# Low parts of q as 128-row operands, and the next pair's stacked operands begun in closer steps

## The chip, the cores and the metric

The kernel runs on one core of one Trainium2 chip. The metric is the device time of one execution in microseconds (us); lower is better. Times shown are medians of several runs. A profile is one further execution with the hardware profiler on; its times are in us from the first instruction.

## The reference, cut to what matters

The reference is one layer of a streaming encoder on 512 prompt frames of one stream and 16 new frames for each of 8 running streams: 640 columns in all, model width 1024. One combined projection gives the input of a state-space branch, q, k, v and two gates. The state-space branch and an attention branch are merged, projected and added to x; a gated feed-forward block with a short convolution follows, then a last norm.

The change lies in the prompt half of the attention: 8 heads of 64 channels, 512 queries. A chunk of 64 queries reads its own and all earlier chunks:

```python
sc = jnp.einsum('nihd,nkhd->nhik', qc, kb).astype(jnp.float32) * scale + bias
sc = jnp.where(valid, sc, MASK_VALUE)
p = jax.nn.softmax(sc, axis=-1).astype(v.dtype)
return jnp.einsum('nhik,nkhd->nihd', p, vb)
```

## The kernel before, in words

**Precision.** TensorE multiplies operands in a reduced fp32 format. To keep fp32 accuracy an operand is split into a high part (ACT rounds it) and a low part (DVE subtracts the high part from the original). A product is then high times high, high times low and low times high.

**Main work and side work.** All instructions are issued in an order fixed when the program is built. The projections run in slots of 8 ticks; one tick is 6 matmuls of 128 rows, 128 columns of weights and 320 moving columns (`mm3`, all of them on line 115). At a slot's first tick the weights three slots on are loaded (`load`, line 100, on SP's queue), the next weights are split on ACT (line 107), and two ticks later on DVE (line 112). The result of the slot before leaves PSUM on DVE (line 1046 for the gates). Ahead of each tick's matmuls a few steps of side work are issued; a rate, `side[2]`, sets how many, about two per tick in the attention. The side work is the state-space branch (`s5`) and then `attention`.

**Attention.** Heads are worked in four pairs. `attention` writes a plan: a list of functions for each step, run in order of step. A pair takes 32 steps. For a pair that begins at step t0, the scores of the eight query blocks (4 tiles of 128 queries, 2 heads) are due at t0, 3, 6, 9, 16, 19, 22 and 25 (`prompt`, function `a`); normalisation follows 4 steps later (`n`, lines 731 and 732), transposes 8 later (`b`, line 738), the product with v 12 after a tile's second head (`prompt_pv`). The running streams' attention (`sample`) is due at steps 12 and 28: its scores (line 786), transposes 8 on (line 802), product with cached v 12 on (line 814). One step after a sample's scores the cached k and v of the next sample are loaded (`load_kv`, lines 769 and 773, three buffers each), on SP's queue. The position bias of the next pair (`load_pb`, line 709, two buffers) is loaded at steps 23 and 26.

**Scores.** A head has 64 channels, so an operand fills 64 of the 128 rows. `stacks` builds, for the next pair, tiles in which the 128 rows are used for two products at once: `ks[:, h2]` holds the high part of k in the head's own 64 rows and its low part in the other 64; `qs[:, h2]` holds the high part of q in both. One 128-row matmul then gives high times high plus high times low. The low part of q lies in `ql` (64 rows of it for each head) and a second matmul of 64 rows adds low times high. Both write PSUM bank `sS`, of which there is one; DVE adds the bias and takes the maximum from it (line 725), after which the next scores may overwrite it. ACT takes the exponent (line 693).

**Building the stacks.** Four functions: the high part of k on ACT (line 663); its low part on DVE (line 668); the copy of that low part to the other 64 rows by two DMAs on SP's queue (line 672), with the high part of q on ACT; the copy of q's high part to the other rows by two DMAs, with q's low part on DVE. They are called at steps 13, 17, 21 and 25 of a pair. For the first pair they run inside `s5`, one in each of its last four rounds.

**SP's queue** issues DMAs in program order; one that waits for a buffer holds those behind it.

At the start of `attention` GpSimd clears `QB` (line 840), a tile for the running streams' q, and DVE copies into it (line 844, two copies in each of four steps), before step 0.

Of the kernel before, what the change touches and what calls it, by code (L numbers as in the profile page):

```python
# [8 lines left out]
F32 = mybir.dt.float32  # L9
F32R = mybir.dt.float32r  # L10
I32 = mybir.dt.int32
AF = mybir.ActivationFunctionType
OP = mybir.AluOpType
# [30 lines left out]
def body(nc, tc, d, ctx):  # L44
# [8 lines left out]
    V, A, G, PE, S = nc.vector, nc.scalar, nc.gpsimd, nc.tensor, nc.sync  # L53
# [3 lines left out]
    def nm(s):  # L57
        uid[0] += 1
        return f"{s}{uid[0]}"

    def ht(dt=F32, w=T):
        return heap.tile([128, w], dt, tag="T", name=nm("h"))
# [4 lines left out]
    def smps(tag):  # L67
        return pss.tile([128, 512], F32, tag=tag, name=nm(tag))
# [45 lines left out]
    def mm(ps, lhs, rhs, start, stop):  # L114
        PE.matmul(ps, lhs, rhs, start=start, stop=stop)  # L115
# [149 lines left out]
    def s5():  # L265
# [359 lines left out]


        first = stacks(0)
        for q in range(4):
            w = w2_ops(q + 2) if q < 2 else []
# [11 lines left out]
    vt_, qT, kT, yh, att = [], [], [], [], []  # L641

    qk = [None]

    def half(h2):
        return slice(64 * h2, 64 * h2 + 64)

    st_ = {}

    def stacks(hp):  # L650


        if hp > 3:
            return []
        k, q, ql = (qk[0].tile([128, n, 512], F32R, tag=t, name=nm(t), bufs=2)
                    for t, n in (("ks", 2), ("qs", 2), ("ql", 1)))
        kl = ht(F32R, 512).rearrange("p (a b) -> p a b", a=1)
        st_[hp] = (k, q, ql)

        def hi(dst, src):  # L660
            for h2 in range(2):
                s = half(h2)
                A.activation(dst[s, h2, :], src[s, 0:512], AF.Copy)

        def lo(dst, src, h):
            for h2 in range(2):
                s = half(h2)
                V.tensor_tensor(dst[s, 0, :], src[s, 0:512], h[s, h2, :].bitcast(F32), op=OP.subtract)

        def move(dst, src):  # L670
            for h2 in range(2):
                S.dma_start(dst[half(1 - h2), h2, :].bitcast(F32), src(h2).bitcast(F32))
        return [lambda: hi(k, kT[hp]), lambda: lo(kl, kT[hp], k),
                lambda: (move(k, lambda h2: kl[half(h2), 0, :]), hi(q, qT[hp])),
                lambda: (move(q, lambda h2: q[half(h2), h2, :]), lo(ql, qT[hp], q))]

    def attention():
        st = ExitStack()
        ap_ = st.enter_context(tc.tile_pool(name="attn", bufs=2))
# [4 lines left out]
        def evac(o, i):  # L684
            cnt[0] += 1
            if cnt[0] % 2:
                A.activation(o, i, AF.Copy)
            else:
                V.tensor_copy(o, i)

        def exps(sb, w, mx):
            V.tensor_scalar(mx[:, 2:3], mx[:, 1:2], -1.0, None, op0=OP.mult)  # L692
            A.activation(sb[:, :w], sb[:, :w], AF.Exp, bias=mx[:, 2:3], accum_out=mx[:, 3:4])  # L693
            return sb

        def tiles():
            sb = ap_.tile([128, T], F32, tag="e", name=nm("sb"), bufs=4)
            mx = ap_.tile([128, 8], F32, tag="mx", name=nm("mx"), bufs=6)
            return sb, mx

        def at(t, fn):
            plan.setdefault(t, []).append(fn)
# [3 lines left out]
        def load_pb(h):  # L706
            if h < 8:
                pbs[h] = ap_.tile([128, 512], F32, tag="pb", name=nm("pb"))
                S.dma_start(pbs[h], d["pbias"][h])

        def prompt(t0, h, t):
            hp, h2 = h // 2, h % 2
            w = 128 * (t + 1)
            s = half(h2)
            m = {}

            def a():
                sc = smps("sS")
                k, q, ql = st_[hp]
                n = max(w, 256)  # L720
                ts = slice(128 * t, 128 * t + 128)
                mm(sc[:, :n], q[:, h2, ts], k[:, h2, 0:n], True, False)
                mm(sc[:, :n], ql[s, 0, ts], k[s, h2, 0:n], False, True)
                sb, mx = tiles()
                V.tensor_tensor_reduce(sb[:, :w], sc[:, :w], pbs[h][:, 512 - w:512], 1.0, -3.0e38,
                                       op0=OP.add, op1=OP.max, accum_out=mx[:, 1:2])
                m["e"], m["mx"] = exps(sb, w, mx), mx

            def n():
                e, mx = m["e"], m["mx"]  # L730
                V.reciprocal(mx[:, 4:5], mx[:, 3:4])
                V.tensor_scalar(e[:, :w], e[:, :w], mx[:, 4:5], None, op0=OP.mult)

            def b():
                e = m["e"]
                pt = smps("sT")
                for k in range(t + 1):
                    PE.transpose(pt[:, k * 128:k * 128 + 128], e[:, k * 128:k * 128 + 128], ident)  # L738
                m["eT"] = ap_.tile([128, 512], F32, tag="eT", name=nm("eT"), bufs=3)
                evac(m["eT"][:, :w], pt[:, :w])  # L740

            at(t0, a)
            at(t0 + 4, n)
            at(t0 + 8, b)
            return m

        def prompt_pv(t0, hp, t, ms):

            def c():
                if t == 0:  # L750
                    po[0] = smps("sP")
                for k in range(t + 1):
                    for h2, m in enumerate(ms):
                        h = 2 * hp + h2
                        mm(po[0][half(h2), 128 * t:128 * t + 128], vt_[k][:, h * 64:h * 64 + 64],
                           m["eT"][:, k * 128:k * 128 + 128], k == 0, k == t)
                if t == 3:
                    evac(att[hp][:, 0:512], po[0])

            at(t0, c)  # L760

        def load_kv(hp, g4):
            if g4 == 0:
                sbs[hp] = ap_.tile([128, 576], F32, tag="sbias", name=nm("sbias"), bufs=1)
                S.dma_start(sbs[hp], d["sbias"][hp])
            kc, vc = [], []
            for i in range(2):
                k = ap_.tile([128, 2, 512], F32, tag="kc", name=nm("kc"), bufs=3)
                S.dma_start(k, d["kc"][hp, g4, :, 2 * i:2 * i + 2])
                kc.append(k)  # L770
            for i in range(2):
                v = ap_.tile([128, 2, 4, 128], F32, tag="vc", name=nm("vc"), bufs=3)
                S.dma_start(v, d["vc"][hp, g4, :, 2 * i:2 * i + 2])
                vc.append(v)
            kvs[hp, g4] = (kc, vc)
# [65 lines left out]
        for hp in range(4):  # L841
            for h2 in range(2):
                s = slice(64 * h2, 64 * h2 + 64)
                V.tensor_copy(QB[s, hp, :, h2, :], qT[hp][s, 512:640].rearrange("p (n i) -> p n i", n=8))
            yield

        t0 = 0
        nxt = [None]
        for hp in range(4):
            for t in range(4):  # L850
                ms = []
                for h2 in range(2):
                    ms.append(prompt(t0, 2 * hp + h2, t))
                    if t == 3:
                        at(t0 + 1, lambda h=2 * hp + h2: load_pb(h + 2))
                    t0 += 3
                    if t == 1 and h2 == 1:
                        at(t0, lambda hp=hp: nxt.__setitem__(0, stacks(hp + 1)))
                        for j in range(4):
                            at(t0 + 1 + 4 * j, lambda j=j: nxt[0] and nxt[0][j]())  # L860
                prompt_pv(t0 - 3 + 12, hp, t, ms)
                if t % 2:
                    i = 2 * hp + t // 2
                    sample(t0, hp, t // 2)
                    if i < 7:
                        at(t0 + 1, lambda i=i: load_kv((i + 1) // 2, (i + 1) % 2))
                    t0 += 4
# [29 lines left out]
    def side_work():  # L897
        qk[0] = qctx.enter_context(tc.tile_pool(name="qk", bufs=1))
        yield from s5()
        side[2] = 172 / (247 - clock[0])  # L900
        yield from attention()
        qctx.close()
# [148 lines left out]
    n = 0  # L1051
# [74 lines left out]
    h2 = xctx2.enter_context(tc.tile_pool(name="heap2", bufs=1))  # L1126
# [298 lines left out]
    for p, nf in enumerate(PARTS):  # L1425
        for j in range(nf):
            f = f0 + j
            q = len(segs)
# [52 lines left out]
    q = len(segs)  # L1481
# [244 lines left out]
```

## Time and profile before

| what | value |
|---|---|
| median of 3 runs | 951.29 us (951.09 to 952.75) |
| profiled execution | 955.98 us, span 953.9 us from first to last instruction |
| mean granted TensorE clock in it | 0.985 of full speed |
| PE busy | 923.4 us, 97% of the span |
| DVE, ACT, POOL busy | 628.0, 442.1 and 133.4 us |
| HBM read, written | 114.56 MB, 8.21 MB |

A row of the timeline is the start in us, the duration in us, the engine, the line, the operation with its output and inputs, for matmuls rows\*columns of the weights and then partitions x moving columns, and how many alike were merged. In brackets stand the idle time of that engine just before and what ended it. Matmuls are pipelined: the step from one start to the next is their price, not their duration.

### The profile page before, as it was taken

How to read it: one execution, taken by the hardware profiler on the slowest of the kernel's cores; microseconds unless marked ns; L12 is line 12 of the kernel's file. 1: busy time of each engine (PE TensorE's matmuls, PEld its weight loads, DVE VectorE, ACT ScalarE, POOL GpSimd, SP SyncE). 2: the span in 40 equal slices, each digit the busy share in tenths (PEclk: the TensorE clock that was granted, in tenths of full speed). 3: DMA queues.
4: the chain of work that ended last, by engine and by line, in shares of the span. 5: the costliest groups of instructions: out<-in, count | busy, mean ns of one | idle time of the engine just before them, and what ended most of it. 6: DMA issues, size and time to landing. Idle time of an engine off the chain costs nothing.

```text
span 953.9 us, 16515 instructions
## 1 busy us (share of the span) xinstructions
PE 923.4 (97%) x6534; PEld 875.8 (92%) x6534; DVE 628.0 (66%) x1261; ACT 442.1 (46%) x689; POOL 133.4 (14%) x228
## 2 busy tenths in 40 slices
PE   8999999999999999999998989999999999999995
PEld 8978999977777799999998989999999999999994
DVE  6783996474665543566777877766766676666545
ACT  6244113343333364433667445545455545555441
POOL 0120403200000000000003212212122211222100
PEclk9999999999999999999999999999999999999998
DMA  6744329666647522234538778889878888899833
GB/s 223 198 137 125 133 68 110 216 199 215 169 129 230 159 81 67 72 105 158 136 84 178 156 165 188 206 186 200 196 178 187 201 191 180 197 191 192 189 57 110
DMA packets 62428, 151.76 MB, mean 159 GB/s; under 512 B 20944, under 2 KB 24208, under 8 KB 62352
## 3 DMA queue, kind: packets, MB, share of 16 engines
q1 hardware_dynamic: 45392, 95.90, 33.3%
q0 software_dynamic: 16096, 54.03, 29.9%
q8 instruction: 51, 0.84, 0.4%
q10 hardware_dynamic: 864, 0.78, 0.2%
q14 instruction: 25, 0.20, 0.1%
HBM read 114.56 MB, written 8.21 MB: 129 GB/s over the span
## 4 chain that ended last, share of the span: by engine, by line
PE 79%; DVE 7%; DMA 6%; ACT 4%; issue 2%; SPq 0%; DVEq 0%; ACTq 0%
PE pb L115 46%; PE sS L115 10%; PE sX L115 8%; PE sT L115 7%; PE sP L115 5%; DMA wl<-in_w 3%; DMA qs<-qs 2%; PE sT L738 1%; DMA fl<-s 1%; PE sX L814 1%; DVE h L1524 1%; DMA wr<-in_w 1%; DVE h L1198 1%; DVE tmp L1356 1%; PE sS L786 1%
## 5 line engine op out<-in xcount | busy, mean ns | idle before, releaser
L115 PE MATMUL pb<-h,wh 128*128 128x320 f32 (+2 forms) x2000 | 389.3, 316 | 4.9 <-ACT h L944 1.8
L115 PEld LDWEIGHTS pb<-h,wh 128*128 128x128 f32 x2000 | 314.2, 190 | 14.3 <-issue 6.6
L115 PE MATMUL pb<-h,wl 128*128 128x320 f32 (+2 forms) x1000 | 231.9, 311 | 0.4 <-DVE wl L112 0.4
L115 PEld LDWEIGHTS pb<-h,wl 128*128 128x128 f32 x1000 | 168.8, 189 | 0.9 <-DVE wl L112 0.7
L1288 POOL DMA_DIRECT2D fl<-s x41 | 35.7, 871 | 455.4 <-PE pb L115 271.8
L107 ACT ACTIVATE wh<-wr 128x1024 fp32r<-128x1024 f32 x50 | 52.7, 1054 | 82.0 <-PE pb L115 55.9
L112 DVE TENSOR_TENSOR wl<-wr,wh 128x1024 fp32r<-128x1024 f32 x50 | 61.1, 1221 | 39.5 <-ACT wh L107 39.3
L115 PE MATMUL sS<-h,wh 128*128 128x320 f32 x336 | 75.6, 312 | 0.0
L115 PE MATMUL sX<-h,fh 128*128 128x320 f32 x320 | 71.7, 312 | 0.0
L1286 ACT ACTIVATE fl<-s 128x1024 fp32r<-128x1024 f32 x41 | 43.3, 1057 | 56.3 <-PE sT L115 48.8
L693 ACT ACTIVATE sb<-sb,mx 128x128 f32<-128x128 f32 (+4 forms) x40 | 24.2, 605 | 73.7 <-DVE mx L692 49.0
L115 PEld LDWEIGHTS sS<-h,wh 128*128 128x128 f32 x336 | 57.0, 190 | 0.0
L115 PE MATMUL sS<-h,wl 128*128 128x320 f32 x168 | 53.0, 316 | 3.1 <-DMA wl<-in_w 3.1
L115 PEld LDWEIGHTS sX<-h,fh 128*128 128x128 f32 x320 | 54.2, 190 | 0.0
L1288 POOL DMA_DIRECT2D wl<-in_w x43 | 38.1, 887 | 87.0 <-ACT wl L1286 79.8
L115 PE MATMUL sX<-h,fl 128*128 128x320 f32 x160 | 49.8, 311 | 0.0
L1359 ACT ACTIVATE tmp<-tmp 128x512 f32<-128x512 f32 x22 | 13.9, 633 | 76.0 <-DVE tmp L1356 76.0
L1286 ACT ACTIVATE wl<-wr 128x1024 fp32r<-128x1024 f32 (+1 forms) x43 | 43.5, 1012 | 7.3 <-PE sS L115 6.2
L115 PE MATMUL sT<-h,gh 128*128 128x320 f32 x176 | 40.0, 315 | 4.5 <-DVE u L1445 4.5
L1287 ACT ACTIVATE wh<-wr 128x1024 fp32r<-128x1024 f32 (+1 forms) x43 | 43.1, 1003 | 0.0
L1287 ACT ACTIVATE fh<-s 128x1024 fp32r<-128x1024 f32 x41 | 42.9, 1046 | 0.0
L1356 DVE SCALAR_TENSOR_TENSOR tmp<-tmp,vec 128x656 f32<-128x656 f32 x44 | 39.5, 898 | 0.7
(338 smaller groups left out, 1684.2 us busy)
## 6 DMA issues: line engine op xcount, KB each, us to landing
wr<-in_w SPq DMA_DIRECT2D x112, 512.0 KB, 4.7
fl<-s POOLq DMA_DIRECT2D x41, 512.0 KB, 6.0
wl<-in_w POOLq DMA_DIRECT2D x39, 512.0 KB, 8.4
kc<-in_kc SPq DMA_DIRECT2D x16, 512.0 KB, 6.4
vc<-in_vc SPq DMA_DIRECT2D x16, 512.0 KB, 5.7
x<-in_x SPq DMA_DIRECT2D x7, 320.0 KB, 6.4
pb<-in_pbias SPq DMA_DIRECT2D x8, 256.0 KB, 7.4
h<-in_x SPq DMA_DIRECT2D x6, 320.0 KB, 4.5
```

Source lines behind the costliest of these rows:

```text
L107: A.activation(hi, raws[u], AF.Copy)
L112: V.tensor_tensor(lo, raws[u], hi.bitcast(F32), op=OP.subtract)
L115: PE.matmul(ps, lhs, rhs, start=start, stop=stop)
L693: A.activation(sb[:, :w], sb[:, :w], AF.Exp, bias=mx[:, 2:3], accum_out=mx[:, 3:4])
L738: PE.transpose(pt[:, k * 128:k * 128 + 128], e[:, k * 128:k * 128 + 128], ident)
L786: PE.matmul(sc[32 * n:32 * n + 32, :], QB[:, hp, 4 * g4 + n].rearrange("p a b -> p (a b)"), kc[n // 2][:, n % 2, :], start=True, stop=True ...
L814: PE.matmul(sx[32 * n:32 * n + 32, 192:320], m["eT"][:, k * 128 + 32 * n:k * 128 + 32 * n + 32], vc[n // 2][:, n % 2, k, :], start=(k == 0 ...
L1286: A.activation(lo, src, AF.Copy, scale=-1.0)
L1287: A.activation(hi, src, AF.Copy)
L1288: G.dma_start(lo, src if again is None else again, accum_op=OP.add)
L1356: V.scalar_tensor_tensor(c_t, a_t[:, j:L + j], vcol(C_CW + 3 * f + j), c_t, op0=OP.mult, op1=OP.add)
L1359: A.activation(g_t[:, 0:512], c_t[:, 0:512], AF.Gelu_apprx_tanh)
```

## The change

`ql` becomes one tile with a half for each head, cleared once at the start of `attention`; only the head's own 64 rows are ever written after that. The second score matmul reads all 128 rows of `ql[:, h2]` and of `ks[:, h2]`; the other 64 rows of `ql` are zero. The subtraction that fills `ql` moves out of `stacks` into `q_low`, which is called behind the first pair's copies into `QB`, and for later pairs at step 28 of the pair before, ahead of that step's sample scores. The four functions of `stacks` are called at steps 13, 15, 17 and 19 instead of 13, 17, 21 and 25.

```diff
-        k, q, ql = (qk[0].tile([128, n, 512], F32R, tag=t, name=nm(t), bufs=2)
-                    for t, n in (("ks", 2), ("qs", 2), ("ql", 1)))
+        k, q = (qk[0].tile([128, 2, 512], F32R, tag=t, name=nm(t), bufs=2) for t in ("ks", "qs"))
         kl = ht(F32R, 512).rearrange("p (a b) -> p a b", a=1)
-        st_[hp] = (k, q, ql)
+        st_[hp] = (k, q)
...
-                lambda: (move(q, lambda h2: q[half(h2), h2, :]), lo(ql, qT[hp], q))]
+                lambda: move(q, lambda h2: q[half(h2), h2, :])]
...
+        ql = ap_.tile([128, 2, 512], F32R, name="ql", bufs=1)
+        for h2 in range(2):
+            G.memset(ql[half(1 - h2), h2, :].bitcast(F32), 0.0)
+
+        def q_low(hp):
+            for h2 in range(2):
+                s = half(h2)
+                V.tensor_tensor(ql[s, h2, :], qT[hp][s, 0:512], st_[hp][1][s, h2, :].bitcast(F32), op=OP.subtract)
...
-                mm(sc[:, :n], ql[s, 0, ts], k[s, h2, 0:n], False, True)
+                mm(sc[:, :n], ql[:, h2, ts], k[:, h2, 0:n], False, True)
...
+            if hp == 0:
+                q_low(0)
             yield
...
-                            at(t0 + 1 + 4 * j, lambda j=j: nxt[0] and nxt[0][j]())
+                            at(t0 + (1, 3, 5, 7)[j], lambda j=j: nxt[0] and nxt[0][j]())
                 prompt_pv(t0 - 3 + 12, hp, t, ms)
+                if t == 3 and hp < 3:
+                    at(t0, lambda hp=hp: q_low(hp + 1))
```

## Rows read from the trace of the kernel before

**Rows 1.** The page, section 1: busy us, share of the span, instructions.

```profile
PE 923.4 (97%) x6534; PEld 875.8 (92%) x6534; DVE 628.0 (66%) x1261; ACT 442.1 (46%) x689; POOL 133.4 (14%) x228
```

**Rows 2.** Timeline, the first scores of pairs two, three and four.

```profile
218.45 0.35 PE L115 MATMUL sS<-ks,qs 128*128 128x256 f32 x1 [1.94 <-DMA qs<-qs]
...
255.84 0.35 PE L115 MATMUL sS<-ks,qs 128*128 128x256 f32 x1 [2.04 <-DMA qs<-qs]
...
292.84 0.36 PE L115 MATMUL sS<-ks,qs 128*128 128x256 f32 x1 [1.59 <-issue]
```

**Rows 3.** Busy time by engine in two stretches; after POOL: PEclk, DMA share, GB/s.

```profile
219.23:222.63 3.40, 3.40 (x13) 2.90 (x13) 1.33 (x6) 2.03 (x4) 0.00 (x0) 0.50 0.91 364
222.64:226.00 3.36, 3.36 (x33) 2.99 (x33) 2.14 (x9) 1.10 (x3) 0.00 (x0) 1.00 0.05 21
```

**Rows 4.** Timeline, PE: projection matmuls, a score of 256 columns, one of 512.

```profile
184.06 0.75 PE L115 MATMUL pb<-h,wh 128*128 128x320 f32 x4
184.64 0.46 PE L115 MATMUL pb<-h,wl 128*128 128x320 f32 x2
...
186.70 0.28 PE L115 MATMUL sS<-ks,qs 128*128 128x256 f32 x1
186.91 0.38 PE L115 MATMUL sS<-ks,ql 64*128 64x256 f32 x1
187.22 0.85 PE L115 MATMUL pb<-h,wh 128*128 128x320 f32 x4
187.90 0.46 PE L115 MATMUL pb<-h,wl 128*128 128x320 f32 x2
...
242.40 0.40 PE L115 MATMUL sS<-ks,qs 128*128 128x512 f32 x1
...
243.84 0.45 PE L115 MATMUL pb<-h,wl 128*128 128x320 f32 x2
```

**Rows 5.** Waits of SP's queue, 180 to 335 us: total us, times, longest.

```profile
SPq L773 <- PE sX L814: 76.7, 7, 11.5
```

**Rows 6.** Timeline of SP's queue ahead of the third pair.

```profile
233.34 12.31 SPq L773 DMA_DIRECT2D vc<-in_vc  x2
245.75 0.38 SPq L100 DMA_DIRECT2D wr<-in_w  x1
246.18 1.10 SPq L672 DMA_DIRECT2D ks<-h  x2
247.38 0.54 SPq L709 DMA_DIRECT2D pb<-in_pbias  x1
248.01 1.12 SPq L672 DMA_DIRECT2D qs<-qs  x2
```

**Rows 7.** The chain of waits: DMAs on it, issue and us to landing.

```profile
211.24 7.08 DMA qs<-qs
248.01 7.69 DMA qs<-qs
```

**Rows 8.** Tile ks, 246 to 252 us: its two copies.

```profile
DMA to landing us min/median/max: 7.1/7.1/7.1
```

**Rows 9.** Tile pb, 247 to 248 us: the bias load.

```profile
DMA to landing us min/median/max: 7.7/7.7/7.7
```

**Rows 10.** Timeline, DVE, first pair, steps 17 to 19.

```profile
201.00 1.40 DVE L668 TENSOR_TENSOR h<-h,ks 64x512 fp32r<-64x512 f32 x2
202.43 0.82 DVE L1046 TENSOR_TENSOR h<-pb,RS 128x640 f32<-128x640 f32 x1
```

**Rows 11.** Timeline, DVE, first pair, step 28: the sample's first reduction.

```profile
212.99 0.69 DVE L791 CUSTOM_DVE_ANT_0 sb<-sS,sbias 128x512 f32<-128x512 f32 x1 [0.90 <-PE sS L786]
```

**Rows 12.** Timeline, POOL and DVE at the start of the attention.

```profile
184.69 0.96 POOL L840 MEMSET QB<- 128x1024 f32 x1
...
185.68 1.87 DVE L844 COPY QB<-h 64x128 f32<-64x128 f32 x8 [6.89 <-DMA pb<-in_pbias]
...
187.58 0.29 DVE L725 CUSTOM_DVE_ANT_0 sb<-sS,pb 128x128 f32<-128x128 f32 x1
```

**Rows 13.** Waits, 183 to 335 us: DVE's reductions of the scores.

```profile
DVE sb L725 <- PE sS L115: 25.3, 19, 3.6
```

More of the change, by code (lines that the diff above doesn't have):

```diff
@@ L713, in prompt @@
             w = 128 * (t + 1)
-            s = half(h2)
             m = {}
@@ L718, in a @@
                 sc = smps("sS")
-                k, q, ql = st_[hp]
+                k, q = st_[hp]
                 n = max(w, 256)
```

## The prediction

> **What bounds the kernel now.** I read the page first: PE is busy 97% of the span [rows 1], so only time taken from PE, or from what PE waits for, counts. The timeline of PE over the attention then shows its idle time there: three gaps of 1.94, 2.04 and 1.59 us, 5.57 in all, each before the first scores of a later pair [rows 2]. Two are put down to the copies of q; the third has the same place. After each gap the granted clock is 0.50 (1.2 of 2.4 GHz) for 3.4 us: 13 matmuls run there where 33 run in the next stretch of that length at full clock [rows 3]. Half of 3.4 us is lost each time, 5.1 us in three. Between the gaps PE is never idle, but the steps between starts are uneven: around each low-part matmul of 64 rows they are too long [rows 4]. The waits show DVE waiting for PE's scores, not the reverse [rows 13]. SP's queue stands still most of the stage, held by a load of cached v that waits for line 814 [rows 5]. So in this stage PE's own steps and one transfer set the time.
>
> **The score matmuls.** Four projection matmuls of 320 columns take 184.64 - 184.06 = 0.58 us, 0.145 each. A score of 256 columns, from its first start past the next four projection matmuls, takes 187.90 - 186.70 = 1.20 us. Less 0.58, its two matmuls cost 0.62 us. If both were full-array, at 0.145 x 256/320 = 0.12 each, they would cost 0.23. The excess of 0.39 has three parts: 0.09 before the low part starts (0.21 for 0.12), 0.19 behind it (0.31 for 0.12), 0.10 in the next four (0.68 for 0.58). A score of 512 columns gives 1.44 - 0.58 = 0.86 against 2 x 0.232 = 0.46, so 0.40 [rows 4]. The price goes with the change of shape and not with the columns. There are 32 scores; 32 x 0.39 = **12.5 us** less on PE. The trace has no 128-row low part. Bounds: if only the part ahead of the low matmul goes, 32 x 0.09 = 3 us; at most 13 us. A loss I exclude, since a 128-row matmul of 320 columns costs 0.145 and a 64-row one of 256 costs 0.31. I take 0.39, because the neighbouring wide matmuls run at 0.145 without exception.
>
> The Trainium skill (TensorEngine Tiling (Array Packing), Key Properties) says that a change of tiling mode drains TensorE. It also says (TensorE: Matmul & The Clock Gate, Part 2) that the drain is about 128 cycles; as an estimate from that page, 64 changes x 53 ns would be 3.4 us, and the whole sum would come to about -6 us and not -15. The trace shows 0.2 us for a change, nearly four times that, so I follow the rows.
>
> **The moves of k and q.** Issued at steps 17 and 19 instead of 21 and 25, they look six steps earlier. They are not: both stand on SP's queue behind the second load of cached v, which program order puts at step 13 and which waits for line 814 at step 24 [rows 5]. What changes is only the order behind it. Ahead of the third pair it was v, weights, k, bias, q [rows 6]; now q goes ahead of the bias. k's second copy landed at 246.74 + 7.1 = 253.8 [rows 6, 8], the bias at 247.38 + 7.7 = 255.1 [rows 9], q's first copy at 255.7 [rows 7], and PE went on at 255.84. Landings follow the order of issue, so taking the bias out brings q forward by about 1.2 us, to 254.5. PE would be ready at 255.84 - 2.04 = 253.8, less 0.4 for the one 512-column score that lies between the release of v and that place: 253.4. A gap of 1.2 us stays. For the fourth pair the same reckoning gives 291.6 against 290.8: 0.8. For the second pair the weights are issued after step 17 and before step 19 (step 17's subtraction precedes the line 1046 that opens the slot [rows 10]), so k passes them and q does not. q's 218.3 [rows 7] falls by 1.2 and at most 0.6 more, to some 216.8, against 218.45 - 1.94 - 0.4 = 216.1: 0.8 with the start.
>
> Then the bias is late next. It lands where q's second copy did, about 256.4 ahead of the third pair. DVE's reduction of the first score waits for it, and the second score, ready 1.6 us after the first, waits for that reduction to leave the one bank `sS`: some 0.6 us there and as much ahead of the second pair. Ahead of the fourth the second score comes a tick later and finds the bias there. The gaps become 1.2 + 0.6, 0.8 + 0.6 and 0.8, 4.0 us instead of 5.57: **-1.6 us**. Bounds: 0 (nothing lands earlier) and -5.6 (all is in time).
>
> **The start.** The first pair's low part of q, made inside `s5` before, now stands behind more. GpSimd clears two halves of 64x512 ahead of `QB`. A clear of 1024 columns took 0.96 us [rows 12]; at half the columns 0.48 each (bounds 0.3 and 0.96). `QB` is then clear at 186.6 instead of 185.65. DVE makes two copies (0.23 each [rows 12]) and two subtractions (0.70 each [rows 10]): the first half is there at 187.8. PE wants it at 186.82, right after the first matmul of the first score: a wait of 1.0. DVE goes on with the second half and six copies to 189.9, and only then reduces the first score (0.29), to 190.2. PE, with one low matmul and six projection matmuls behind it, wants `sS` at 188.9: a wait of 1.3. Together **+2.4 us**, with bounds of 1 and 4. Nothing hides these: PE works in order, and until then every tick ahead of the scores was full.
>
> **The clock.** It fell after gaps of 1.59 us and more; the gaps that I leave are of 0.6 to 1.3 us, two of them close together at three places. At four places it may fall, and I take one fall of 1.7 us: 5.1 - 1.7 = **-3.4 us**. Bounds: -5.1 and +1.7.
>
> **Edits at no cost.** `q_low` for a later pair puts 1.4 us on DVE ahead of the sample's reduction at 212.99, which follows 0.90 us of idle time [rows 11]: 0.5 us later, and the next user of `sS` comes over 2 us on; without that cover 3 x 0.5. The same 1.4 us goes from step 25, where it stood ahead of another reduction. k's subtraction two steps earlier waits for ACT and moves one reduction back by 0.7 us, ahead of a score some 2.5 us on; without cover 3 x 0.4. ACT's part for q falls between exponents. Weights land two slots before use.
>
> **The sum.** -12.5 - 1.6 + 2.4 - 3.4 = -15.1 us. On the profiled execution, 955.98 us with a span of 953.9, that is 940.9. All terms lie in the attention, and PE is full behind it, so the same is taken from the median of 951.29: **936.2 us**. The profiled execution is 4.7 us above the median; if timed runs miss some of the clock's falls, less is to be had back, up to 5 us.
>
> **Rivals.**
> *All transfers in time, start hidden in part.* If k and q land by their need, the gaps go whole and with them the falls: -12.5 - 5.6 - 5.1 + 2.4 = -20.8, 930.5 us. For it: the moves precede the bias. Against: SP is held until line 814. Chance 0.15.
> *The clock still falls everywhere.* The start's two waits and the left gaps drop it four times: -12.5 - 1.6 + 2.4 + 1.7 = -10.0, 941.3 us. For it: 1.8 us of idle time in two pieces ahead of the third pair. Against: no row shows a fall after so short a gap. Chance 0.17.
> *Only part of the switch goes.* The excess behind the low part stays, because it belongs to loading the next weights: -3 - 1.6 + 2.4 - 3.4 = -5.6, 945.7 us. The skill's drain would give about the same. Against: weight loads between wide matmuls show no excess. Chance 0.10.
> *Slower: `sS` sets the pace.* If each score waited for DVE to empty the one bank, shorter matmuls would only lengthen PE's idle time: 0 for the first term, 0 for the gaps, +2.4 for the start and one more fall, +1.7: +4.1, 955.4 us. It decides where DVE's work between scores exceeds PE's. Against: DVE waited 25.3 us for scores, 19 times [rows 13]. Chance 0.05.
> The forecast has the rest, 0.53, with a range of its own of 933 to 939.
>
> **How the numbers follow.** 0.2% of 951 is 1.9 us, about what a measurement of this kernel tells from no change. The first three cases and the forecast are all faster by more. With something left for a mechanism that I don't see: faster 0.93, same 0.03, slower 0.04. The range reaches past the first two rivals and leaves out most of the other two: 929 to 943.5.
>
> **What would show it.** Right: the low part's rows read 128\*128, a score of 256 columns reaches the next four projection matmuls' end in 0.82 us; cached v still holds SP until line 814; q is issued ahead of the bias and about 1.2 us earlier against line 814; idle time of PE appears at the first and second score of the first pair. Wrong: steps of 0.3 behind the low part stay, or the copies of q land before PE's need. The prediction fails as a whole if PE's idle time in the attention grows by more than 10 us.

## The result, and the profile after

The changed kernel takes 940.53 us (median of 4 runs, 940.0 to 943.39) against 952.02 us for the kernel before on the same chip (4 runs, 951.09 to 953.64). The ratio is 0.9894, with an interval of 0.9874 to 0.9914: 10.1 us faster (8.2 to 12.0). The two medians alone differ by 11.5 us; the accounts below go by the ratio. The forecast was 936.2 us with a range of 929 to 943.5; the time is in the range, but 4.3 us above the forecast and outside the likeliest case's own 933 to 939.

The profiled execution took 940.75 us (span 938.9, clock 0.993). That is 15.2 us below the profiled execution of before, almost exactly the predicted sum, and misleading: the execution of before that was profiled was 4.7 us above its own median. In it the clock stood at 0.50 five times between 100 and 900 us; in that of after twice. Two of the five lay behind the attention, where the change does nothing.

The page of after, section 1, answers to [rows 1]:

```profile
PE 906.8 (97%) x6534; PEld 868.9 (93%) x6534; DVE 627.1 (67%) x1261; ACT 441.5 (47%) x689; POOL 134.4 (14%) x230
```

The two kernels issue the same 6534 matmuls in the same order, so a stage can be cut at the same matmuls in both. Busy time by engine from the first to the last high-part score of the attention (length; then PE, PEld, DVE, ACT, POOL, PEclk, DMA share, GB/s), before:

```profile
186.70:320.15 133.45, 127.66 (x1040) 98.67 (x1039) 80.26 (x266) 50.97 (x122) 0.00 (x0) 0.96 0.60 188
```

and after:

```profile
185.67:307.75 122.08, 114.37 (x1040) 94.87 (x1039) 81.92 (x272) 50.48 (x122) 0.00 (x0) 0.99 0.63 205
```

The stage is 11.4 us shorter, PE's busy time in it 13.3 us less, and its idle time (length less busy) went up from 5.8 to 7.7 us. Laid matmul against matmul over the stage and a little beyond (-11.8 us in all), the steps at the scores at full clock gave -10.0, PE's waits of over 0.25 us +2.1 (7.69 against 5.57), the steps with the clock at 0.50 in either kernel -3.7, the rest -0.1.

**Scores.** Timeline of PE after, a score of 256 columns with the projection matmuls behind it, answers to [rows 4]:

```profile
293.56 0.28 PE L115 MATMUL sS<-ks,qs 128*128 128x256 f32 x1
293.67 0.28 PE L115 MATMUL sS<-ks,ql 128*128 128x256 f32 x1
293.79 0.75 PE L115 MATMUL pb<-h,wh 128*128 128x320 f32 x4
294.38 0.46 PE L115 MATMUL pb<-h,wl 128*128 128x320 f32 x2
```

The low part reads 128\*128 and the four matmuls end 294.38 - 293.56 = 0.82 us after the score's start, as forecast; it was 1.20.

**The start.** PE after, the first two scores:

```profile
185.67 0.28 PE L115 MATMUL sS<-ks,qs 128*128 128x256 f32 x1
186.94 0.36 PE L115 MATMUL sS<-ks,ql 128*128 128x256 f32 x1 [0.99 <-issue]
...
189.35 0.58 PE L115 MATMUL sS<-ks,qs 128*128 128x256 f32 x1 [1.18 <-DVE mx L733]
```

and what stands in front of them on POOL and DVE, answering to [rows 12]:

```profile
183.66 1.10 POOL L698 MEMSET ql<- 64x512 f32 x2
184.70 0.94 POOL L848 MEMSET QB<- 128x1024 f32 x1
...
185.68 0.46 DVE L852 COPY QB<-h 64x128 f32<-64x128 f32 x2 [8.62 <-POOL QB L848]
186.15 1.40 DVE L703 TENSOR_TENSOR ql<-h,qs 64x512 fp32r<-64x512 f32 x2
187.57 1.40 DVE L852 COPY QB<-h 64x128 f32<-64x128 f32 x6
189.00 0.29 DVE L733 CUSTOM_DVE_ANT_0 sb<-sS,pb 128x128 f32<-128x128 f32 x1
```

Two waits of 0.99 and 1.18 us, each at the foretold instruction. The clock fell behind them, the one fall that is left in the stage (two stretches, columns as above).

```profile
185.85:189.26 3.41, 1.33 (x8) 1.00 (x7) 3.24 (x12) 0.00 (x0) 0.00 (x0) 1.00 0.97 360
189.27:192.68 3.41, 3.33 (x13) 3.33 (x14) 1.52 (x8) 3.11 (x6) 0.00 (x0) 0.50 1.03 408
```

**The later pairs.** The first scores of pairs two, three and four after, answering to [rows 2]:

```profile
216.98 0.36 PE L115 MATMUL sS<-ks,qs 128*128 128x256 f32 x1 [0.28 <-DMA qs<-qs]
...
250.95 0.36 PE L115 MATMUL sS<-ks,qs 128*128 128x256 f32 x1 [1.65 <-DMA qs<-qs]
...
283.28 0.35 PE L115 MATMUL sS<-ks,qs 128*128 128x256 f32 x1 [1.41 <-DMA qs<-qs]
```

SP's queue ahead of the third pair, answering to [rows 6]:

```profile
228.90 12.66 SPq L781 DMA_DIRECT2D vc<-in_vc  x2
241.65 0.38 SPq L100 DMA_DIRECT2D wr<-in_w  x1
242.09 1.11 SPq L672 DMA_DIRECT2D ks<-h  x2
243.28 1.19 SPq L672 DMA_DIRECT2D qs<-qs  x2
244.57 1.12 SPq L718 DMA_DIRECT2D pb<-in_pbias  x2
```

q is ahead of the bias now, but goes out 1.6 us behind the weights' load that follows the released load of v (243.28 against 241.65), where it went 2.3 us behind it before [rows 6]: 0.6 us gained, not 1.2. And two waits are new. PE waits for a copy of exponents twice in the sample's transposes:

```profile
235.56 0.65 PE L810 MATMUL sT<-ident,sb 128*128 128x128 f32 x4 [1.42 <-ACT eT L687]
...
287.23 0.66 PE L810 MATMUL sT<-ident,sb 128*128 128x128 f32 x4 [0.76 <-ACT eT L687]
```

The first has k's subtraction behind it. DVE and then ACT ahead of it:

```profile
231.36 1.40 DVE L668 TENSOR_TENSOR h<-h,ks 64x512 fp32r<-64x512 f32 x2 [0.66 <-ACT ks L663]
232.79 0.56 DVE L733 CUSTOM_DVE_ANT_0 sb<-sS,pb 128x384 f32<-128x384 f32 x1
...
233.58 0.62 ACT L693 ACTIVATE sb<-sb,mx 128x384 f32<-128x384 f32 x1 [1.60 <-DVE mx L692]
...
234.20 1.04 ACT L107 ACTIVATE wh<-wr 128x1024 fp32r<-128x1024 f32 x1
235.14 0.36 ACT L687 ACTIVATE eT<-sT 128x256 f32<-128x256 f32 x1
```

The subtraction waits for ACT's high part and holds the reduction; so the exponent starts late, behind it ACT's split of the weights (1.04 us) and only then the copy that frees bank `sT`. The second comes from the bias, late now as the forecast had it, in another place: DVE's first reduction of the fourth pair waits for it, the exponent on ACT waits for the reduction, and the copy that frees `sT` comes behind the exponent:

```profile
285.62 0.29 DVE L733 CUSTOM_DVE_ANT_0 sb<-sS,pb 128x128 f32<-128x128 f32 x1 [3.64 <-DMA pb<-in_pbias]
...
286.20 0.40 ACT L693 ACTIVATE sb<-sb,mx 128x128 f32<-128x128 f32 x1 [4.29 <-DVE mx L692]
...
286.60 0.58 ACT L687 ACTIVATE eT<-sT 128x512 f32<-128x512 f32 x1
```

### The profile page after: what moved, and what is told of

It is laid out like the page before. It is cut to its first block, busy times and chain, and to the rows that moved or that the text cites. A ratio compares the mean times of both kernels' runs of the same rounds, so it can differ in the third digit from the quotient of the medians.

```text
span 938.9 us, 16523 instructions
## 1 busy us (share of the span) xinstructions
PE 906.8 (97%) x6534; PEld 868.9 (93%) x6534; DVE 627.1 (67%) x1261; ACT 441.5 (47%) x689; POOL 134.4 (14%) x230
## 4 chain that ended last, share of the span: by engine, by line
PE 72%; DMA 9%; DVE 7%; ACT 5%; issue 4%; POOL 1%; SPq 1%; DVEq 0%; POOLq 0%; ACTq 0%
PE pb L115 40%; PE sS L115 9%; PE sT L115 7%; PE sX L115 7%; PE sP L115 5%; DMA wl<-in_w 3%; DMA o_s<-SV 2%; DMA qs<-qs 1%; DMA fl<-s 1%; DMA pb<-in_pbias 1%; PE sX L822 1%; DVE h L1536 1%; DMA wr<-in_w 1%; ACT wh L107 1%; PE sT L746 1%
## 5 line engine op out<-in xcount | busy, mean ns | idle before, releaser
L115 PE MATMUL pb<-h,wh 128*128 128x320 f32 (+2 forms) x2000 | 384.4, 313 | 4.7 <-DVE h L1517 1.2
```

## The experiments

Each ratio is against runs of the kernel before on the same chip, whose medians were 950.6 to 950.9 us. Below, "the stage" is from the first to the last high-part score, in the profile. "..." in an edit marks lines left out.

**One part of the change at a time.** The first keeps the 128-row low part and puts the four building steps back:

```diff
-  at(t0 + (1, 3, 5, 7)[j], ...)
+  at(t0 + (1, 5, 9, 13)[j], ...)
```

> The 128-row low parts and their place (q_low at the start and at step 28), with the stacks' four functions back at steps 13, 17, 21 and 25. My theory: the shape of the low part carries the gain and the closer steps little. Scores keep steps of 0.12 us at 256 columns, some 12 us less in all; the gaps ahead of the later pairs' first scores stay at 1.6 to 2.4 us and drop the clock two or three times; the 1.4 us wait of the second pair's sample transposes (line 810) goes, since k's subtraction is back at step 17; the start costs 2.2 us and perhaps a fall. About 942 to 946 us against 952 of before. Rival, the closer steps are worth most: over 947. Rival, they cost as much as they bring: the same as the changed kernel, 940.5.

Measured: 941.19 us, ratio 0.9902 (0.9877 to 0.9927). That is just below the 942 to 946 expected. The gaps ahead of the three pairs were 1.60, 2.35 and 3.38 us, the stage 125.87 us, 3.8 longer than after (2.3 of waits, 1.8 at the lower clock), but the sample's transposes in the second pair waited 0.46 instead of 1.42 us. The timed runs do not tell it from the changed kernel. The second is the kernel before, with the closer steps alone (the same line, changed to 13, 15, 17, 19):

> The kernel before with the closer steps alone (13, 15, 17, 19); low parts stay 64-row operands and are made with q's copies at step 19. My theory: SP's queue holds the copies until line 814 whatever their step, so q's copies land only about 1 us earlier, one or two of the three falls of the clock stay, and the wait for ACT by k's earlier subtraction turns up at line 802. 949 to 952.5 us. Rival, the closer steps bring the copies in time: gaps and falls go, 942 to 945 us.

Measured: 948.17 us, ratio 0.9966 (0.9948 to 0.9985), the stage 126.11. The time lies between the two forecasts, 0.8 us below the first. Against before: PE's idle time -2.8 us, steps at the lower clock -4.5. The gaps were 0.85 (the transposes), 1.07 and 0.91, and no fall stands in the stage. So the shape carries the gain that is timed. The steps alone are worth some 3 us by the timed runs (7.3 in the two profiles, 4.5 of it clock), and their wait at the transposes takes a part back.

**The start.** Of the changed kernel, the first low part of q ahead of the copies into `QB`, and `QB` cleared before the zero rows of `ql`:

```diff
-        for h2 in range(2):
-            G.memset(ql[half(1 - h2), h2, :].bitcast(F32), 0.0)
         ...
+        q_low(0)
         ...
         G.memset(QB, 0.0)
+        for h2 in range(2):
+            G.memset(ql[half(1 - h2), h2, :].bitcast(F32), 0.0)
         ...
-            if hp == 0:
-                q_low(0)
```

> The changed kernel with another order at the start of the attention: the first pair's low part of q is made on DVE ahead of the copies into QB, and GpSimd clears QB before the zero rows of ql. My theory: PE's waits of 0.99 and 1.18 us at the first two scores and the fall of the clock behind them go: 2.2 us less, or 3.9 with the fall; 936.5 to 938.5 against 940.5 of the changed kernel. Rival, DVE and ACT are late there in any case (table load, first exponents) and the waits come back within the next scores: no difference, 940.5.

Measured: 935.47 us, ratio 0.9852 (0.9825 to 0.9879). The first of the two waits is gone and the second is 0.69 us. The stage is 121.19, only 0.9 shorter than after: in this profiled execution the fall of the clock moved from the start to 249.78, behind the gap ahead of the third pair (1.91 us). The later gaps grew by 0.7 us in all. So the start's order costs 1.5 us of waiting by the profile; the timed runs show 4 to 5 us. About 2 us more stand in their granted clocks, 0.994 on the mean against 0.992 of the changed kernel's; the rest is not settled.

**The queue.** Of the changed kernel, the second load of cached v of each sample one step behind the product that frees its buffer:

```diff
         ...
         at(t0 + 1, lambda i=i: load_kv((i + 1) // 2, (i + 1) % 2))
+        at(t0 + 13, lambda i=i: load_v((i + 1) // 2, (i + 1) % 2, 1))
```

> The changed kernel with the second load of a sample's cached v issued one step after the product that frees its buffer (step 25 and 41 of a pair) and not at step 13 or 29, so that nothing on SP's queue stands behind its wait. My theory: the copies of k and q are issued at their steps, land some 4 us earlier and PE's gaps ahead of the second to fourth pairs (0.28, 1.65 and 1.41 us) go, with the late bias behind the fourth: 3.3 to 4 us less, 936.5 to 937.5, and no fall of the clock there. The wait at line 810 of the second pair (1.4 us) stays. Rival, the transfers are late because the DMA engines are full then, and not for SP's order: gaps stay within 0.5 us of theirs, 940 to 941.

Measured: 935.29 us, ratio 0.9842 (0.9816 to 0.9867), the stage 115.25. The gaps ahead of pairs two, three and four are gone, whole; the start's two waits (0.98 and 1.19) and the transposes' 1.42 remain, and no fall of the clock is left in the stage. The third pair's first score follows without a gap:

```profile
247.87 0.45 PE L115 MATMUL pb<-h,wl 128*128 128x320 f32 x2
248.15 0.28 PE L115 MATMUL sS<-ks,qs 128*128 128x256 f32 x1
```

The time from issue to landing of q's copies (min, median, max) between 200 and 300 us, in the changed kernel:

```profile
DMA to landing us min/median/max: 5.9/7.4/7.7
```

and with v later:

```profile
DMA to landing us min/median/max: 2.2/3.0/3.4
```

So the held load of v cost twice: it kept k and q from being issued, and once released, its transfer and that of the weights behind it ran ahead of theirs. The Trainium skill (DMA: Bandwidth & Descriptors, Queues, rings and completion order) says that each DMA engine consumes the descriptors of one issuing queue in ring order; the trace agrees, 7.4 us behind v's load and 3.0 without it.

**The shape by itself.** To price it without gaps or falls, the kernel before (64-row low parts, its own steps) with v loaded at step 25:

> The kernel before (low parts of q of 64 rows, building steps 13, 17, 21, 25), with only the second load of cached v at step 25 instead of 13. Theory: cached v on SP's queue made all three gaps; without it the gaps (5.6 us) and their falls of the clock go, 941 to 944, and the later v with the change (935.3) is 7 to 9 us below it: the 128-row form (10 to 12.5 us) less the start (2.2 us). Rival: the copies of q issued at step 25 take over 7 us and come too late even with a free queue; then gaps of about 1 us stay ahead of pairs 2 to 4, with falls, and the time is 946 to 949.

Measured: 942.05 us, ratio 0.9911 (0.9889 to 0.9932); not one gap of PE over 0.25 us in the stage and the clock at full speed throughout:

```profile
186.63:309.30 122.67, 122.45 (x1041) 94.61 (x1039) 80.02 (x266) 50.87 (x122) 0.00 (x0) 1.00 0.60 205
```

This is the cleanest stage of 64-row scores. It has the old building steps: with the queue free, copies of q called at step 25 are in time, and the closer steps are not needed for it (with 64-row low parts; with 128-row ones, where PE is sooner there, it was not run). Against the kernel with all three edits (below), which has 128-row ones and the clock at full speed too, the score steps alone differ by 11.7 us, matmul by matmul: 0.37 each for 32. Then the same kernel with each 64-row low part issued twice (low times high is added twice):

```diff
+                mm(sc[:, :n], ql[s, 0, ts], k[s, h2, 0:n], False, False)
                 mm(sc[:, :n], ql[s, 0, ts], k[s, h2, 0:n], False, True)
```

> The kernel before with the second load of cached v at step 25 (no gaps in the attention, 942 us), in which each score issues its 64-row low part twice, so that low times high is added twice. Theory: the price of 0.37 us goes with the change of shape between 64 and 128 rows, so a second 64-row matmul in a row costs its columns alone: 352 columns on average at 0.145 per 320, 0.16 us, x 32 = 5.1 us: 946 to 949. Rival: every 64-row matmul is slow by itself (0.31 us for 256 columns): 32 x 0.31 to 0.4 = 10 to 13 us, 952 to 955.

Measured: 949.01 us, at the upper end of the forecast, ratio 0.9971 (0.9957 to 0.9986); the stage 127.16, 4.49 longer for 32 more matmuls, 0.14 each. (The timed difference is 6 to 7 us; outside the stage its profiled execution has two falls of the clock, the other none.) The first score, once:

```profile
186.63 0.28 PE L115 MATMUL sS<-ks,qs 128*128 128x256 f32 x1
186.84 0.38 PE L115 MATMUL sS<-ks,ql 64*128 64x256 f32 x1
187.15 0.85 PE L115 MATMUL pb<-h,wh 128*128 128x320 f32 x4
```

and twice:

```profile
186.16 0.28 PE L115 MATMUL sS<-ks,qs 128*128 128x256 f32 x1
186.37 0.50 PE L115 MATMUL sS<-ks,ql 64*128 64x256 f32 x2
186.80 0.85 PE L115 MATMUL pb<-h,wh 128*128 128x320 f32 x4
```

From the low part's start to the projection it is 0.31 with one and 0.43 with two: the second 64-row matmul costs 0.12 us, what 256 columns cost at 128 rows. It is the change of shape that costs, not the 64 rows. By the Trainium skill (TensorEngine Tiling (Array Packing), Key Properties) a change of mode drains TensorE: the trace agrees that a change costs, 0.37 us for the way there and back by the two stages compared above.

**The transposes' wait.** Of the changed kernel, the second building step at 17 again, the others right behind it:

```diff
-  at(t0 + (1, 3, 5, 7)[j], ...)
+  at(t0 + (1, 5, 6, 7)[j], ...)
```

> The changed kernel with its second building step (k's subtraction on DVE) back at step 17 and the other two at 18 and 19. Theory: the wait of 1.42 us of the sample's transposes in the second pair comes from k's subtraction at step 15, which waits for ACT's high part and holds the reduction behind it; with it at step 17 that wait goes, the gaps ahead of pairs 3 and 4 stay (about 1.6 and 1.4 us), and the time falls by 1 to 2 us, to 939 to 940. Rival: ACT's split of the weights alone makes the copy of the exponents late; then the wait stays at 1.4 us at the same place and the time is within 0.5 us of the changed kernel's 940.5.

Measured: 940.26 us, ratio 0.9889 (0.9867 to 0.9911). The wait fell from 1.42 to 0.47 us, and the 0.76 in the fourth pair went too, but the gap there grew from 1.41 to 1.94. The stage is 119.57, 2.5 shorter, which the timed median does not show. The mechanism is as foreseen, apart from the 0.47, which is not the step's: the first experiment, with all steps back, has 0.46. A gain in time is not shown, and by the time alone the rival (within 0.5 us of 940.5) holds.

**All three together.** The start's order, the later v and this step:

> The changed kernel with three edits: the first low part of q ahead of the copies into QB, the second load of cached v at step 25 instead of 13, and the building steps 13, 17, 18, 19. Theory (the waits that are left are three separate causes and add up): the start's two waits shrink to 0.7 us, the gaps ahead of pairs 2 to 4 and the wait of the sample's transposes go, no fall of the clock in the attention: 5 us from the start and 5.5 us from cached v below 940.5, and 1.4 us more from the step: 928 to 931. Rival (the causes share their gain, since the clock's falls that each removes are the same ones): no more than 2 us better than the later v alone, 933 to 935.

Measured: 932.3 us, ratio 0.9806 (0.9777 to 0.9834), between the two forecasts. The run meant to bring back the steps of the change beside it,

> As the kernel with three edits, but with the building steps of the change (13, 15, 17, 19). Theory of separate causes: 930 to 932, and 1 to 2 us above the one with the step moved, with one wait of about 1.4 us ahead of the sample's transposes in the second pair. Rival: the wait of the transposes is an accident of the start's time and is gone or stands elsewhere; then the two are within 0.5 us of one another.

was built without that edit, so it is the same kernel again: 931.3 us, ratio 0.9795 (0.9777 to 0.9813). The 8 runs together have a median of 931.3. The stage of the first:

```profile
185.94:298.28 112.34, 111.18 (x1041) 93.36 (x1039) 80.27 (x269) 50.62 (x122) 0.09 (x1) 1.00 0.67 224
```

Idle time in it is 1.2 us (0.69 at the start, 0.47 at the transposes), against 7.7 after. The transposes:

```profile
231.06 0.66 PE L810 MATMUL sT<-ident,sb 128*128 128x128 f32 x4 [0.47 <-ACT eT L687]
```

The causes are separate as far as the waits go: each went with its own edit. The missing edit was made in a later run:

> The changed kernel with the first low part of q ahead of the copies into QB and the second load of cached v at step 25, and with the building steps of the change (13, 15, 17, 19). Theory: k's subtraction at step 15 holds DVE's reduction ahead of the second pair's transposes again, so that wait is 1.4 us where it is 0.5 with the step at 17, and the time is about 1 us above that kernel's 931 to 932. Rival: where the wait stands depends on where the tick's weights fall, which both other edits move; then it stays at 0.5 us and the two are within 0.5 us.

Measured: 934.02 us, ratio 0.9820 (0.9795 to 0.9845), the stage 113.55. The wait is back at full size:

```profile
231.92 0.66 PE L810 MATMUL sT<-ident,sb 128*128 128x128 f32 x4 [1.42 <-ACT eT L687]
```

It is 0.95 us longer than with the step at 17, and the stage 1.2: k's subtraction two steps earlier made it, whatever the start and the queue do. The times' intervals overlap; the trace decides this one.

**What was left of the start.** Of the kernel with three edits, the copies into `QB` at steps 2, 4, 6 and 8:

```diff
         ...
         for hp in range(4):
+            at(2 + 2 * hp, lambda hp=hp: qb(hp))
```

> The best kernel so far (low part of q ahead, cached v at step 25, k's subtraction at step 17) with DVE's eight copies into QB moved from ahead of step 0 to steps 2, 4, 6 and 8, two in each. Theory: the 0.70 us that PE still waits for the first reduction is DVE's 2.6 us of copies; it goes, the copies (0.65 us a pair) find idle time of DVE between later scores, and the time falls by 0.5 to 0.9 us. Rival: the copies hold a later reduction by 0.65 us each and the single score bank gives it back: no change or up to 2 us more.

Measured: 930.36 us, ratio 0.9775 (0.9751 to 0.9800); the stage 112.40 against 112.34. The 0.69 us ahead of the second score went, and 0.49 appeared at the fourth. PE at the fourth, then DVE ahead of it:

```profile
190.83 0.39 PE L115 MATMUL sS<-ks,qs 128*128 128x256 f32 x1 [0.49 <-DVE mx L731]
...
189.86 0.45 DVE L856 COPY QB<-h 64x128 f32<-64x128 f32 x2
190.34 0.42 DVE L731 CUSTOM_DVE_ANT_0 sb<-sS,pb 128x256 f32<-128x256 f32 x1
```

The copies hold a later reduction instead: the rival's mechanism, in the stage no gain. Its time is the lowest of all, but its interval overlaps that of the kernel with three edits, and its runs had a higher granted clock (0.995 to 0.997 against 0.991 to 0.996). Either beats both the kernel before and the changed one, by some 20 and 10 us.

## Why the prediction was right or wrong

**Scores, -12.5: right.** Measured without disturbance -11.7 (0.37 each for 0.39), and the reason, the change of shape and not the columns, held against its rival in the run with doubled low parts. The rival "only part of the switch goes" is out: all three parts of the excess went.

**The start, +2.4: right in the waits** (0.99 and 1.18 for 1.0 and 1.3). The clock behind them fell, where the forecast had counted one fall of four places without naming which.

**Gaps of k and q, -1.6: right in the sum by luck, wrong pair by pair.** The order behind the load of v was right, but taking the bias out brought q's issue forward by 0.6 us and not 1.2: the landings were taken as one after another, while what moved was one DMA's issue. So the gaps ahead of the third and fourth pairs stayed at 1.65 and 1.41 us where 1.2 and 0.8 were foreseen. At pair two k passed the weights, as said, and the gap shrank to 0.28 where 0.8 was foreseen. The bias was late, as said, but held PE by 0.76 us at the fourth pair, and not by 0.6 at the second and third. These errors cancel: gaps and bias came to 4.10 us, against 4.0 foreseen and 5.57 before, -1.5.

**Edits at no cost: the step failed in one.** k's subtraction was priced at "0.7 us, ahead of a score some 2.5 us on". It was ahead of more: the reduction it holds releases an exponent, behind which ACT has the weights' split and the copy that frees `sT`. The cover was looked for on DVE and at `sS`; it ended on ACT. This wait is 1.42 us, which the sum had at 0; 0.95 of it is due to the step, and what makes the other 0.47 was not isolated.

**The clock, -3.4: right in the profile, too large for the timed runs.** In the stage three falls became one, as taken. But the term was read from one execution with a mean clock of 0.985; the 41 later runs of the same kernel have 0.987 to 0.993, so most have fewer falls to give back. The prediction named this ("up to 5 us") and did not put it into the sum. With scores -11.7, gaps and bias -1.5, the start +2.2 and the subtraction +1.4, the measured -10.1 leaves about -0.5 to the clock, by the two medians -1.9. A check from the granted clocks of the timed runs (span times what the clock lacks of full speed, an estimate) gives 8.6 us lost on the mean in the 41 runs of before and 7.8 in the four of after: -0.9. All are far from -3.4. By the ratio, this term's 2.9 us, the subtraction's 1.4, the scores' 0.8 and the gaps' 0.1, less 0.2 at the start, are the 5.0 us by which the change fell short of -15.1.

**Rivals.** "All transfers in time" needed the queue free: with v later the gaps went whole. "The clock still falls everywhere" foretold 941.3, nearest to the time, but by another road: one fall in the stage, not four. "Slower" never came near: PE waited for bank `sS` once, for 1.18 us at the start.

## What to carry to other kernels

A matmul of fewer rows between full ones paid here for changing the shape twice, 0.37 us; try padding it with zero rows, if the zeros can be set once. Before moving a step earlier, look at what its queue is held by at that place, and follow what the moved instruction delays across engines to the next bank that must come free. And take what is to be had from the clock over several executions, not from the one that was profiled.

## What the runs showed of the hardware

A gap's length did not settle whether the clock fell: after 1.59 us ahead of the fourth pair it did before [rows 2], after 1.65 us ahead of the third it did not in the changed kernel, after 2.35 us in the first experiment neither:

```profile
252.57 0.35 PE L115 MATMUL sS<-ks,qs 128*128 128x256 f32 x1 [2.35 <-DMA qs<-qs]
```

A second 64-row matmul directly behind another cost 0.12 us for 256 columns, and a lone one between 128-row matmuls 0.37 us more than a 128-row one.
